# The table that turns S5 inputs into states, formed with steps and channels on the partitions instead of with states on the partitions and transposed afterwards

## The chip, the cores and the metric

The kernel runs on one core of a Trainium2 chip. The metric is the device time of one execution in microseconds (us). TensorE (PE) does the matrix products and the transposes, VectorE (DVE) and ScalarE (ACT) the work on elements, GpSimd (POOL) in this kernel mostly issues DMAs, and SyncE (SP) issues the loads of the weights. Each engine works through its own list of instructions in order; where one needs what another engine or a DMA makes, it waits on a semaphore.

## The reference

One inference step of a backbone of two layers (`DEPTH = 2`) with 1024 channels over 384 tokens, 128 of context and 256 latent. In each layer two half-step feed-forward networks (hidden width 2816) stand around a mixing block. One branch of the mixing block is a linear state-space layer (S5): 32 groups of 16 channels, each with 64 complex states, in both directions of time. Cut to it:

```python
def _s5_direction(u, a_re, a_im, log_dt, b_re, b_im, c_re, c_im, h0, reverse):
    dt = jnp.exp(log_dt)[:, None]
    mag = jnp.exp(a_re * dt)
    abar_r, abar_i = mag * jnp.cos(a_im * dt), mag * jnp.sin(a_im * dt)
    ...                                      # q = (abar - 1) / a
    bbar_r = qr[..., None] * b_re - qi[..., None] * b_im
    bbar_i = qr[..., None] * b_im + qi[..., None] * b_re
    bu_r = jnp.einsum('gph,blgh->blgp', bbar_r, u)
    ...
    _, _, sr, si = lax.associative_scan(_ssm_combine, (ar, ai, bu_r, bu_i), reverse=reverse, axis=1)
    y = jnp.einsum('ghp,blgp->blgh', c_re, sr) - jnp.einsum('ghp,blgp->blgh', c_im, si)
```

The scan is linear, so the kernel takes eight steps (`TC = 8`) of a group's 16 channels (`H`) at once, 128 numbers, and needs three tables for each group: one from the eight steps' inputs to the 128 states of both directions (`ms`, products of powers of `abar` with `bbar`), one from the states to the eight outputs (`my`, powers with `c`), and one from inputs to outputs inside the eight steps (`kall`, spread out to `mi`). None of the tables depends on the tokens; only the weights enter.

## The kernel before

**The stream of weights.** Every projection is cut into units of 512 KB (four blocks of 128 rows by 256 columns). SP loads a unit (`wr`), ACT copies its high part into `wh` (L126), DVE subtracts to get the low part `wl` (L105), and PE does three products for each block, 24 matrix products a unit (`mm3`, L198 to L200). The pool of `wh` and `wl` has three buffers, so the `wh` of unit u+3 cannot be written before PE has finished unit u, and `next_unit` asks for the unit two ahead (`LOOK = 2`, L173). I number the units of the program from 0; the layers' first feed-forward network, in which layer 0's tables are made, takes units 0 to 67.

**What sets the order.** PE's list is in the order in which the code is written (L61). The lists of DVE, ACT, POOL and SP are ordered by a scheduler when the program is built; the weights' copies and subtractions have a higher priority there. After each unit `tick()` (L221) lets side programs go on by some steps: each is a Python generator, and what stands between two of its `yield`s is written into the program at that place. The side programs make the modulation vectors (`ax<-modw`, L386, with `modev` copies, L396) and the S5 tables. The tables' program goes on by 1.9 steps a unit in layer 0 and by 1.6 in layer 1.

**The tables.** `s5_params` (L788) forms the powers `pw` of `abar` and writes them in two orders to DRAM (`px`). `s5_tables` (L924) treats a layer's 32 groups in four rounds of eight (`GB`), each in two halves of four (`GS`). A round transposes `cr`, scales `braw` to `bb` (four products `cm` and two sums), and copies `bb` into the zero-padded `bp`. A half then makes `my` in six DVE operations of 128x512, and `mt`, the to-state table with the states on the partitions, in six more. Three steps later come the half's PE work: the responses (`tb<-my,bp`, L1024, and L1034, copied to `kall`, L1042) and eight transposes of `mt` (L138), which ACT copies to `ms` (L1050). POOL issues the DMAs of all of this: 33 in a round (8 loads, 2 of `my`, 2 of `ms`, 12 of `kall`, 9 that spread it to `mi`).

Of the kernel before, what the change touches and what calls it, by code (L numbers as in the profile page):

```python
# [19 lines left out]
P = 128  # L20
# [14 lines left out]
G = 32  # L35
# [21 lines left out]
def hybrid_step(ctx: ExitStack, tc: tile.TileContext, I, pos_r, pos_c, y_prompt, y_sample, new_state):  # L57
# [31 lines left out]
    def c4(shape, name):  # L89
        return sp.tile(shape, F32, tag="c4", name=name, bufs=5)  # L90
# [4 lines left out]
    def c2(shape, name):  # L95
        return sp.tile(shape, F32, tag="c2", name=name, bufs=7)
# [4 lines left out]
    def s1(shape, name):  # L101
        return sp.tile(shape, F32, tag="s1", name=name, bufs=7)
# [616 lines left out]
    px_d = [drm.tile([P, 2, 2, TC, G], F32, tag=f"px{l}", name=f"px{l}") for l in range(DEPTH)]  # L719
# [68 lines left out]
    def s5_params(raw, ldt):  # L788
# [81 lines left out]
        lo_i = slice(TC - 1, None, -1), slice(1, TC + 1)  # L870
        hi_i = slice(0, TC), slice(TC, 0, -1)
        for w in range(2):
            px = c4([P, DEPTH, 2, TC, G], "px")
            for i in range(2):
                for rows, ix in ((LO, lo_i[w]), (HI, hi_i[w])):
                    src = pw[rows, i, ix, :].rearrange("p n (l g) -> p l n g", l=DEPTH)
                    for l in range(DEPTH):
                        act.activation(px[rows, l, i], src[:, l], AF.Copy)
            for l in range(DEPTH):
                q.dma_start(px_d[l][:, w], px[:, l])  # L880
# [43 lines left out]
    def s5_tables(l):  # L924
        q = nc.gpsimd
        px = []
        for w in range(2):
            t = c2([P, 2, TC, G], "pxl")
            q.dma_start(t, px_d[l][:, w])
            px.append(t)  # L930
        psx, pyx = px
# [18 lines left out]
        for gb in range(G // GB):  # L950
# [9 lines left out]
            pool.memset(bb, 0.0)  # L960
# [5 lines left out]
            pool.memset(bp, 0.0)  # L966
# [4 lines left out]
            ts_(nci, cT[:, 1], -1.0)  # L971
            if gb + 1 < G // GB:
                nxt = load_bc(gb + 1)
            kall = s1([P, 2, 9 * H], "kall")
            for sb in range(GB // GS):
                s0 = sb * GS

                def pexp(tab, i):
                    v = tab[:, i, :, g0 + s0 : g0 + s0 + GS]
                    return v.rearrange("p n g -> p g n").unsqueeze(3).to_broadcast(sh)  # L980
# [5 lines left out]
                b_r, b_i = vec(bb[:, 0]), vec(bb[:, 1])  # L986
                my = c4([P, GS, 2, TC, H], "my")
                t1, t2 = c2(sh, "tp1"), c2(sh, "tp2")
                mul(t1, pexp(pyx, 0), c_r)
                mul(t2, pexp(pyx, 1), c_i)  # L990
# [3 lines left out]
                mul(t1, pexp(pyx, 1), c_r)  # L994
                yield
                mul(t2, pexp(pyx, 0), c_i)
# [10 lines left out]
                mt = c4([P, GS, 2, TC, H], "mt")  # L1007
                t1, t2 = c2(sh, "tp1"), c2(sh, "tp2")
                mul(t1, pexp(psx, 0), b_r)
                mul(t2, pexp(psx, 1), b_i)  # L1010
                yield
                sub(mt[:, :, 0], t1, t2)
                t1, t2 = c2(sh, "tp1"), c2(sh, "tp2")
                mul(t1, pexp(psx, 0), b_i)
                yield
                mul(t2, pexp(psx, 1), b_r)
                add(mt[:, :, 1], t1, t2)
                for _ in range(3):
                    yield
# [833 lines left out]
```

## Time and profile before

| | us |
|---|---|
| median of three runs | 1774.3 (1772.38 to 1775.49) |
| the profiled execution's own time | 1775.03 |
| its span in the trace | 1773.0 |
| PE busy | 1743.7 (98%) |
| DVE busy | 1246.8 (70%) |
| ACT busy | 795.8 (45%) |
| POOL busy | 203.5 (11%) |
| PE's waits for the subtraction `wl` | 4.2, in 5 waits |
| mean granted clock of TensorE | 0.997 |

The span is the time from the first to the last record; the execution's own time is 2.03 us longer. Busy shares are means over the whole program. PE's records are modelled at their ends and overlap, so that the step from one start to the next, and not the length of a record, tells how long a matrix product holds the engine: here 0.17 to 0.18 us, so that a unit of 24 takes about 4.1 us.

### The profile page before, as it was taken

What the parts mean: (1) busy time and instruction counts of PE and PEld (TensorE: products, weight loads), DVE (VectorE), ACT (ScalarE), POOL (GpSimd) and SP (SyncE); (2) the same over time, 40 slices, a digit from 0 to 9 for tenths busy, and PEclk for the clock granted to TensorE, in tenths of its full rate; (3) what the DMA queues carried; (4) which work ended last, traced back from release to release, by engine and by line L of the source; (5) the groups of instructions that cost most, each with busy time, mean ns of one, the idle gap of its engine ahead of it and who ended that gap; (6) DMA issues with size and microseconds to landing.
All of it is one profiled execution on the core that took longest, in us unless ns stands there. A gap on an engine that the chain in (4) does not pass through costs nothing.

```text
span 1773.0 us, 30946 instructions
## 1 busy us (share of the span) xinstructions
PE 1743.7 (98%) x12116; PEld 1652.8 (93%) x12116; DVE 1246.8 (70%) x2344; ACT 795.8 (45%) x1330; POOL 203.5 (11%) x400
## 2 busy tenths in 40 slices
PE   7999999999999999999999999999999999999997
PEld 4899999999999989999999899999999999999997
DVE  5496676778986885678487666767799788544435
ACT  3344333575355553233366233336744546423233
POOL 2012343310010000000001133232100000000000
PEclk9999999999999999999999999999999999999999
DMA  9778788776753677788346776667666443444332
GB/s 343 249 224 275 231 252 269 226 198 190 240 157 108 186 238 228 237 280 257 112 131 208 234 224 215 175 195 233 162 210 200 131 123 116 132 130 127 123 125 77
DMA packets 253753, 344.48 MB, mean 194 GB/s; under 512 B 22399, under 2 KB 216651, under 8 KB 253608
## 3 DMA queue, kind: packets, MB, share of 16 engines
q1 hardware_dynamic: 228504, 299.18, 53.4%
q0 software_dynamic: 17088, 39.51, 7.5%
q10 hardware_dynamic: 8016, 3.82, 0.8%
q8 instruction: 95, 1.56, 0.4%
q14 instruction: 50, 0.41, 0.1%
HBM read 309.75 MB, written 32.70 MB: 193 GB/s over the span
## 4 chain that ended last, share of the span: by engine, by line
PE 81%; DVE 10%; ACT 4%; DMA 3%; issue 2%; SPq 0%; ACTq 0%; DVEq 0%
PE mm L198 25%; PE mm L200 25%; PE mm L199 25%; PE ax L386 3%; DVE wl L105 3%; DVE cacc L123 2%; DMA wr<-in_w_gate_dram 1%; DVE m_t L105 1%; PE tb L138 1%; ACT wh L126 1%; DVE m_hh L105 1%; DMA modw<-in_w_mod_dram 1%; DVE macc L123 1%; DMA wr<-in_w_in_dram 1%; ACT zp L1125 0%
## 5 line engine op out<-in xcount | busy, mean ns | idle before, releaser
L105 DVE TENSOR_TENSOR wl<-wr,wh 128x1024 fp32r<-128x1024 f32 (+2 forms) x389 | 457.0, 1175 | 352.1 <-ACT wh L126 347.4
L126 ACT ACTIVATE wh<-wr 128x1024 fp32r<-128x1024 f32 (+1 forms) x387 | 395.9, 1023 | 613.9 <-PE mm L199 443.9
L198 PE MATMUL mm<-hh,wh 128*128 128x384 f32 x1840 | 625.3, 340 | 2.7 <-ACT hh L621 2.7
L200 PE MATMUL mm<-hh,wl 128*128 128x384 f32 x1840 | 617.1, 335 | 4.4 <-DVE wl L105 4.2
L199 PE MATMUL mm<-hl,wh 128*128 128x384 f32 x1840 | 616.3, 335 | 0.5 <-DVE hl L105 0.3
L198 PEld LDWEIGHTS mm<-hh,wh 128*128 128x128 f32 x1840 | 345.9, 188 | 31.7 <-issue 18.1
L200 PEld LDWEIGHTS mm<-hh,wl 128*128 128x128 f32 x1840 | 345.8, 188 | 6.7 <-DVE wl L105 6.7
L199 PEld LDWEIGHTS mm<-hl,wh 128*128 128x128 f32 x1840 | 345.9, 188 | 1.2 <-DVE hl L105 1.1
L198 PE MATMUL mm<-ah,wh 128*128 128x384 f32 x800 | 273.2, 342 | 0.0
L199 PE MATMUL mm<-al,wh 128*128 128x384 f32 x800 | 269.4, 337 | 0.8 <-DVE al L105 0.8
L200 PE MATMUL mm<-ah,wl 128*128 128x384 f32 x800 | 270.0, 338 | 0.0
L198 PEld LDWEIGHTS mm<-ah,wh 128*128 128x128 f32 x800 | 150.2, 188 | 10.2 <-issue 6.7
L199 PEld LDWEIGHTS mm<-al,wh 128*128 128x128 f32 x800 | 150.4, 188 | 1.7 <-DVE al L105 1.1
L200 PEld LDWEIGHTS mm<-ah,wl 128*128 128x128 f32 x800 | 150.2, 188 | 0.0
L123 DVE SCALAR_TENSOR_TENSOR x<-mm,gt,x 128x128 f32<-128x128 f32 x224 | 83.1, 411 | 33.3 <-PE mm L200 33.1
L198 PE MATMUL mm<-xh,wh 128*128 128x386 f32 x240 | 84.7, 353 | 0.0
L126 ACT ACTIVATE ah<-av 128x384 fp32r<-128x384 f32 x82 | 42.1, 519 | 89.4 <-DVE av L105 89.1
L200 PE MATMUL mm<-xh,wl 128*128 128x386 f32 x240 | 81.9, 341 | 0.0
L199 PE MATMUL mm<-xl,wh 128*128 128x386 f32 x240 | 81.9, 341 | 0.0
L123 DVE SCALAR_TENSOR_TENSOR macc<-modw,silu_c,macc 128x1024 f32<-128x1024 f32 x56 | 69.9, 1278 | 14.9 <-DMA modw<-in_w_mod_dram 14.9
L123 DVE SCALAR_TENSOR_TENSOR cacc<-pad,pv,cacc 128x399 f32<-128x399 f32 x120 | 69.7, 627 | 0.0
L386 PE MATMUL ax<-modw,silu_c 128*32 128x512 f32 (+1 forms) x576 | 63.2, 511 | 0.7 <-DMA modw<-in_w_mod_dram 0.7
(316 smaller groups left out, 1820.0 us busy)
## 6 DMA issues: line engine op xcount, KB each, us to landing
wr<-in_ffn_w_dram SPq DMA_DIRECT2D x256, 512.0 KB, 3.6
modw<-in_w_mod_dram SPq DMA_DIRECT2D x144, 512.0 KB, 5.4
wr<-in_w_gate_dram SPq DMA_DIRECT2D x48, 512.0 KB, 3.8
wr<-in_w_in_dram SPq DMA_DIRECT2D x24, 512.0 KB, 3.6
my<-my POOLq DMA_DIRECT2D x16, 512.0 KB, 5.5
ms<-ms POOLq DMA_DIRECT2D x16, 512.0 KB, 4.9
m_ms<-ms SPq DMA_DIRECT2D x16, 512.0 KB
m_my<-my SPq DMA_DIRECT2D x16, 512.0 KB, 7.4
```

The lines of the kernel that those rows point to most:

```text
L105: (eng or dve).tensor_tensor(out, a, b, op=op)
L123: dve.scalar_tensor_tensor(out, a, s, b, op0=op0, op1=op1)
L126: act.activation(hi, full, AF.Copy)
L138: pe.transpose(out, in_, ident[:rows, :rows])
L198: pe.matmul(out, wh[:, k, cols], xh, start=first, stop=False)
L199: pe.matmul(out, wh[:, k, cols], xl, start=False, stop=False)
L200: pe.matmul(out, wl[:, k, cols], xh, start=False, stop=last)
L386: pe.matmul(b[32 * s : 32 * s + 32, :w], silu_c[:, k, :], raws[i][:, c : c + w], start=(k == 0), stop=(k == KD - 1), skip_group_check=True,)
```

## The change

The to-state table is no longer transposed; its factors are. Once for the program, `pw` is transposed (eight transposes, four ACT copies into `pws`) and written to DRAM (`pt_d`, eight DMAs). In each round `factor_rows` copies `bb` to `bc` on ACT, transposes it (two transposes), copies the result to `bts` on ACT and writes it eight times to DRAM, once for each step (`btr_d`). In each half `to_rows_in` reads the powers with each row repeated for 16 partitions (`pt`, eight DMAs of 64 KB) and the repeated `bts` (`bt`, one DMA of 512 KB), and `to_rows` multiplies them on DVE in six operations of 128x512, straight into `ms`. The zeros of `bb` and `bp` are written by DVE in place of POOL, and only where they are needed. The second order of the powers (`psx`) is gone, and the `s1` pool has nine buffers instead of seven. POOL's DMAs in a round go from 33 to 59. A round has 16 steps instead of 17; the responses of a half come one or two steps after its `my` (before, at least five), and the factor's transposes three steps after `bb` is written into the program.

```diff
     def s1(shape, name):
-        return sp.tile(shape, F32, tag="s1", name=name, bufs=7)
+        return sp.tile(shape, F32, tag="s1", name=name, bufs=9)
...
-    px_d = [drm.tile([P, 2, 2, TC, G], F32, tag=f"px{l}", name=f"px{l}") for l in range(DEPTH)]
+    px_d = [drm.tile([P, 2, TC, G], F32, tag=f"px{l}", name=f"px{l}") for l in range(DEPTH)]
+    pt_d = [drm.tile([2, TC, G, P], F32, tag=f"pt{l}", name=f"pt{l}") for l in range(DEPTH)]
+    btr_d = [drm.tile([TC, H, G, 2 * P], F32, tag=f"btr{l}", name=f"btr{l}") for l in range(DEPTH)]
...
+        pws = c4([P, TC, P], "pws")
+        for i in range(2):
+            b = tb_bank()
+            for m in range(TC // 2):
+                transpose(
+                    b[:, m * P : (m + 1) * P], pw[:, i, 2 * m : 2 * m + 2, :].rearrange("p n r -> p (n r)"), P
+                )
+            bv = b.rearrange("p (m s) -> p m s", s=P)
+            o = pws[:, 4 * i : 4 * i + 4]
+            act.activation(o[:, ::-1, LO], bv[:, :, LO], AF.Copy)
+            act.activation(o[:, :, HI], bv[:, :, HI], AF.Copy)
+            yield
+        for n2 in range(2):
             for l in range(DEPTH):
-                q.dma_start(px_d[l][:, w], px[:, l])
+                r = n2 * NG + l * G
+                rows_d = pt_d[l].rearrange("i j g s -> (i j) g s")
+                for half, off in ((LO, 1 - n2), (HI, n2)):
+                    q.dma_start(
+                        rows_d[off::2, :, half].rearrange("m g s -> g m s"), pws[r : r + G, :, half]
+                    )
         yield
...
             bb = c2([P, 2, GB, 2 * H], "bb")
-            pool.memset(bb, 0.0)
+            dve.memset(bb[:, :, :, H:], 0.0)
...
             bp = c2([P, 2, GB, 2 * H], "bp")
-            pool.memset(bp, 0.0)
+            dve.memset(bp[LO, :, :, H:], 0.0)
+            dve.memset(bp[HI, :, :, :H], 0.0)
...
             nci = s1([P, GB, H], "nci")
             ts_(nci, cT[:, 1], -1.0)
+            bc = s1([P, 2, GB, H], "bc")
+            act.activation(bc, bb[:, :, :, :H], AF.Copy)
             if gb + 1 < G // GB:
                 nxt = load_bc(gb + 1)
+
+            def factor_rows():
+                b = tb_bank()
+                for i in range(2):
+                    transpose(b[:, i * P : (i + 1) * P], bc[:, i].rearrange("p g h -> p (g h)"), P)
+                bts = s1([P, 2, P], "bts")
+                act.activation(bts.rearrange("p i s -> p (i s)"), b[:, : 2 * P], AF.Copy)
+                for j in range(TC):
+                    q.dma_start(btr_d[l][j, :, gs].rearrange("h g x -> g h x"), bts.rearrange("r i s -> r (i s)"))
+
...
-                mt = c4([P, GS, 2, TC, H], "mt")
-                t1, t2 = c2(sh, "tp1"), c2(sh, "tp2")
-                mul(t1, pexp(psx, 0), b_r)
-                mul(t2, pexp(psx, 1), b_i)
+
+            def to_rows_in(sb):
+                gr = slice(g0 + sb * GS, g0 + (sb + 1) * GS)
+                pt = c4([P, 2, GS, P], "pt")
+                for j in range(TC):
+                    q.dma_start(pt[j * H : (j + 1) * H], pt_d[l][:, j, gr].unsqueeze(0).to_broadcast([H, 2, GS, P]))
+                bt = c4([P, GS, 2 * P], "bt")
+                q.dma_start(bt, btr_d[l].rearrange("j h g x -> (j h) g x")[:, gr])
+                bt = bt.rearrange("p g (i s) -> p g i s", s=P)
+                ins.append((pt, bt))
+
+            def to_rows(sb):
+                pt, bt = ins[sb]
+                ms = c4([P, GS, 2, P], "ms")
+                t1, t2 = (c2([P, GS, P], f"tp{i}") for i in (1, 2))
+                mul(t1, pt[:, 0], bt[:, :, 0])
+                mul(t2, pt[:, 1], bt[:, :, 1])
                 yield
-                sub(mt[:, :, 0], t1, t2)
-                t1, t2 = c2(sh, "tp1"), c2(sh, "tp2")
-                mul(t1, pexp(psx, 0), b_i)
+                sub(ms[:, :, 0], t1, t2)
+                t1, t2 = (c2([P, GS, P], f"tp{i}") for i in (1, 2))
+                mul(t1, pt[:, 0], bt[:, :, 1])
                 yield
-                mul(t2, pexp(psx, 1), b_r)
-                add(mt[:, :, 1], t1, t2)
-                for _ in range(3):
-                    yield
+                mul(t2, pt[:, 1], bt[:, :, 0])
+                add(ms[:, :, 1], t1, t2)
+                q.dma_start(ms_d[l][:, g0 + sb * GS : g0 + (sb + 1) * GS], ms)
+                yield
...
                 act.activation(kall[:, sb, :], b[:, : 9 * H], AF.Copy)
-                ms = c4([P, GS, 2, P], "ms")
-                for g2 in range(0, GS, 2):
-                    b = tb_bank()
-                    for j in range(4):
-                        transpose(
-                            b[:, j * P : (j + 1) * P], mt[:, g2 + j // 2, j % 2].rearrange("p i h -> p (i h)"), P
-                        )
-                    act.activation(ms[:, g2 : g2 + 2].rearrange("p g r c -> p (g r c)"), b, AF.Copy)
-                q.dma_start(ms_d[l][:, g0 + s0 : g0 + s0 + GS], ms)
+
+            mys, ins = [], []
+            yield
+            for n, _ in enumerate(from_rows(0)):
+                if n == 1:
+                    factor_rows()
+                yield
+            for n, _ in enumerate(from_rows(1)):
+                if n == 0:
+                    responses(0)
+                yield
+            to_rows_in(0)
+            yield
+            responses(1)
+            yield
+            to_rows_in(1)
+            yield from to_rows(0)
+            yield from to_rows(1)
             for s in range(4):
                 r = 32 * s
```

**Where the order differs on PE.** First the end of a half in before: the matrix products of `modw` belong to the modulation vectors, the rest to the tables.

```order
L386 MATMUL ax<-modw,silu_c 32x512 x4
L1024 MATMUL tb<-my,bp 32x128 x8
L1034 MATMUL tb<-cT,bb 32x16 x4
L1034 MATMUL tb<-nci,bb 32x16 x4
L138 MATMUL tb<-ident,mt 128x128 x8
L198 MATMUL mm<-ah,wh 128x384
```

In after, the responses stand alone at their place, and the transposes of a round come earlier. This is the place in layer 0's last round; the matrix product above it is the last of unit 54.

```order
L200 MATMUL mm<-hh_377,wl 128x384
L386 MATMUL ax<-modw,silu_c 32x512 x4
L138 MATMUL tb<-ident,bc 128x128 x2
L198 MATMUL mm<-hh_523,wh 128x384
L199 MATMUL mm<-hl_524,wh 128x384
```

The eight transposes of `mt` are gone from every half; two transposes of `bc` stand once in a round, directly behind a unit.

**Where the order differs on DVE.** Layer 0's last round, before: the scaling of `braw` (L105; `cm` are the products).

```order
L105 TENSOR_TENSOR wl<-wr,wh 128x1024
L105 TENSOR_TENSOR cm_3369<-q_t,braw 128x128
L105 TENSOR_TENSOR cm_3370<-q_t,braw 128x128
L105 TENSOR_TENSOR cm_3374<-q_t,braw 128x128
L105 TENSOR_TENSOR bb<-cm_3369,cm_3370 128x8x16
L105 TENSOR_TENSOR cm_3375<-q_t,braw 128x128
L105 TENSOR_TENSOR wl<-wr,wh 128x1024
L105 TENSOR_TENSOR bb<-cm_3374,cm_3375 128x8x16
```

The same place in after. The first row is the subtraction for unit 57, the unit three behind the one that PE finishes ahead of the transposes of `bc`.

```order
L105 TENSOR_TENSOR wl<-wr,wh 128x1024
L105 TENSOR_TENSOR ms<-tp_3219,tp_3220 128x4x128
L105 TENSOR_TENSOR ms<-tp_3260,tp_3261 128x4x128
L105 TENSOR_TENSOR tp_3297<-pt,bt 128x512
L105 TENSOR_TENSOR tp_3298<-pt,bt 128x512
L105 TENSOR_TENSOR tp_3302<-pt,bt 128x512
L105 TENSOR_TENSOR ms<-tp_3297,tp_3298 128x4x128
L105 TENSOR_TENSOR tp_3303<-pt,bt 128x512
L977 MEMSET bb 128x16x16
L105 TENSOR_TENSOR ms<-tp_3302,tp_3303 128x4x128
L105 TENSOR_TENSOR bb<-cm_3419,cm_3420 128x8x16
L105 TENSOR_TENSOR bb<-cm_3424,cm_3425 128x8x16
```

The sums that make `bb` now stand behind the subtraction for unit 57 and behind nine rows of the previous half's `ms`, where before they stood between two subtractions. ACT's copies into `bp` (four) and `bc`, which the transposes wait for, follow them; they stand behind ACT's copy `wh` for unit 57 as well.

## Rows read from the trace of the kernel before

**Rows 1.** The page: its head, busy times, and the chain by engine.
```profile
span 1773.0 us, 30946 instructions
...
PE 1743.7 (98%) x12116; PEld 1652.8 (93%) x12116; DVE 1246.8 (70%) x2344; ACT 795.8 (45%) x1330; POOL 203.5 (11%) x400
...
PE 81%; DVE 10%; ACT 4%; DMA 3%; issue 2%; SPq 0%; ACTq 0%; DVEq 0%
```

**Rows 2.** PE's waits: what for, us in total, times, longest.
```profile
PE ax L138 <- DMA crow<-in_c_dram: 5.3, 1, 5.3
PE mm L200 <- DVE wl L105: 4.2, 5, 1.4
...
PE ax L138 <- ACT modev L396: 0.5, 1, 0.5
```

**Rows 3.** Timeline of PE at a half's end: start, us, engine, line, names.
```profile
179.55 0.23 PE L1034 MATMUL tb<-nci,bb 128*32 128x16 f32 x8
179.71 1.24 PE L138 MATMUL tb<-ident,mt 128*128 128x128 f32 x8
180.71 0.42 PE L198 MATMUL mm<-hh,wh 128*128 128x384 f32 x1
```

**Rows 4.** Timeline of PE around a pair of transposes.
```profile
159.42 0.34 PE L200 MATMUL mm<-hh,wl 128*128 128x384 f32 x1
159.59 0.38 PE L138 MATMUL tb<-ident,cr 128*128 128x128 f32 x2
159.73 0.42 PE L198 MATMUL mm<-hh,wh 128*128 128x384 f32 x1
159.99 0.33 PE L199 MATMUL mm<-hl,wh 128*128 128x384 f32 x1
```

**Rows 5.** Timeline of PE, ACT and DVE at one unit's end.
```profile
173.37 0.34 PE L200 MATMUL mm<-hh,wl 128*128 128x384 f32 x1
173.62 1.06 ACT L126 ACTIVATE wh<-wr 128x1024 fp32r<-128x1024 f32 x1 [1.46 <-PE mm L199]
173.64 1.06 PE L386 MATMUL ax<-modw,silu_c 128*32 128x512 f32 x8
...
174.71 1.23 DVE L105 TENSOR_TENSOR wl<-wr,wh 128x1024 fp32r<-128x1024 f32 x1
```

**Rows 6.** DVE groups by shape: busy us, mean ns, idle before.
```profile
L105 DVE TENSOR_TENSOR wl<-wr,wh 128x1024 fp32r<-128x1024 f32 x355 | 433.7, 1222 | 318.2 <-ACT wh L126 313.4 <-PE ax L386 3.1
...
L105 DVE TENSOR_TENSOR tp<-pxl,bb 128x512 f32<-128x512 f32 x64 | 42.5, 685 | 0.4
...
L105 DVE TENSOR_TENSOR mt<-tp,tp 128x512 f32<-128x512 f32 x32 | 21.9, 685 | 0.2
...
L105 DVE TENSOR_TENSOR cm<-q_t,braw 128x128 f32<-128x128 f32 x32 | 7.8, 286 | 14.1 <-PE tb L138 10.1 <-DMA kd<-kall 4.0
...
L105 DVE TENSOR_TENSOR bb<-cm,cm 128x128 f32<-128x128 f32 x16 | 4.5, 284 | 0.0
```

**Rows 7.** ACT groups by shape.
```profile
L1050 ACT ACTIVATE ms<-tb 128x512 f32<-128x512 f32 x32 | 18.0, 599 | 2.5 <-PE tb L138 2.5
...
L969 ACT ACTIVATE bp<-bb 64x128 f32<-64x128 f32 x16 | 4.9, 307 | 0.2
...
L396 ACT ACTIVATE modev<-ax 128x512 f32<-128x512 f32 x5 | 2.9, 590 | 0.5 <-PE ax L386 0.5
L958 ACT ACTIVATE cT<-tb 128x256 f32<-128x256 f32 x8 | 2.9, 368 | 0.9 <-PE tb L138 0.9
```

**Rows 8.** Timeline of PE after a wait, with the idle time before it.
```profile
360.61 0.37 PE L468 MATMUL ax<-ones,sqacc 128*32 128x1 f32 x24 [1.96 <-DVE sqacc L105]
...
361.62 0.53 PE L198 MATMUL mm<-xh,wh 128*128 128x386 f32 x1
361.94 0.53 PE L199 MATMUL mm<-xl,wh 128*128 128x386 f32 x1
...
364.52 0.49 PE L198 MATMUL mm<-xh,wh 128*128 128x386 f32 x1
364.84 0.34 PE L199 MATMUL mm<-xl,wh 128*128 128x386 f32 x1
```

**Rows 9.** Windows: us, busy PE, PEld, DVE, ACT, POOL; PEclk, DMA share, GB/s.
```profile
362.00:364.00 2.00, 2.00 (x8) 2.00 (x7) 2.00 (x6) 0.00 (x0) 0.00 (x0) 0.50 0.66 198
```

**Rows 10.** The same view, layer 0's tables.
```profile
250.00:280.00 30.00, 30.00 (x210) 26.89 (x203) 26.08 (x48) 9.20 (x16) 13.81 (x25) 1.00 0.88 279
```

**Rows 11.** POOL groups by shape.
```profile
L1059 POOL DMA_DIRECT2D mib<-kd x64 | 33.6, 533 | 14.6 <-DMA kd<-kall 6.8 <-PE mm L200 3.3 <-issue 2.9
...
L1054 POOL DMA_DIRECT2D kd<-kall x32 | 16.5, 516 | 109.4 <-ACT kall L1042 102.8 <-DMA ms<-ms 6.5 <-issue 0.2
...
L942 POOL DMA_DIRECT2D cr<-in_s_c_re_dram x16 | 9.0, 566 | 4.1 <-DMA mib<-kd 2.1 <-DVE tp L105 1.8 <-issue 0.2
...
L960 POOL MEMSET bb<- 128x512 f32 x8 | 4.3, 532 | 20.2 <-DVE mt L105 20.2
```

**Rows 12.** DMA issues: KB each, median us to landing.
```profile
my<-my POOLq DMA_DIRECT2D x16, 512.0 KB, 5.5
ms<-ms POOLq DMA_DIRECT2D x16, 512.0 KB, 4.9
...
mib<-kd POOLq DMA_DIRECT2D x64, 64.0 KB, 5.6
```

More of the change, by code (lines that the diff above doesn't have):

```diff
@@ L868, in s5_params @@
             yield
[L870 to L878, printed above, removed]
-            for l in range(DEPTH):
-                q.dma_start(px_d[l][:, w], px[:, l])
+        px = c4([P, DEPTH, 2, TC, G], "px")
+        for i in range(2):
+            for rows, ix in ((LO, slice(1, TC + 1)), (HI, slice(TC, 0, -1))):
+                src = pw[rows, i, ix, :].rearrange("p n (l g) -> p l n g", l=DEPTH)
+                for l in range(DEPTH):
+                    act.activation(px[rows, l, i], src[:, l], AF.Copy)
+        for l in range(DEPTH):
+            q.dma_start(px_d[l], px[:, l])
+        yield
[12 more added lines that the diff above has]
+        for n2 in range(2):
+            for l in range(DEPTH):
+                r = n2 * NG + l * G
[4 more added lines that the diff above has]
+                    )
         yield
@@ L925, in s5_tables @@
         q = nc.gpsimd
[L926 to L931, printed above, removed]
+        pyx = c2([P, 2, TC, G], "pxl")
+        q.dma_start(pyx, px_d[l])
         def load_bc(gb):
@@ L971, in s5_tables, with from_rows, pexp @@
             ts_(nci, cT[:, 1], -1.0)
+            bc = s1([P, 2, GB, H], "bc")
+            act.activation(bc, bb[:, :, :, :H], AF.Copy)
             if gb + 1 < G // GB:
                 nxt = load_bc(gb + 1)
+            def factor_rows():
+                b = tb_bank()
+                for i in range(2):
+                    transpose(b[:, i * P : (i + 1) * P], bc[:, i].rearrange("p g h -> p (g h)"), P)
[3 more added lines that the diff above has]
+                    q.dma_start(btr_d[l][j, :, gs].rearrange("h g x -> g h x"), bts.rearrange("r i s -> r (i s)"))
             kall = s1([P, 2, 9 * H], "kall")
-            for sb in range(GB // GS):
+            def from_rows(sb):
                 s0 = sb * GS
-                def pexp(tab, i):
-                    v = tab[:, i, :, g0 + s0 : g0 + s0 + GS]
+                def pexp(i):
+                    v = pyx[:, i, :, g0 + s0 : g0 + s0 + GS]
                     return v.rearrange("p n g -> p g n").unsqueeze(3).to_broadcast(sh)
@@ L985, in s5_tables @@
                 c_r, c_i = vec(cT[:, 0]), vec(cT[:, 1])
-                b_r, b_i = vec(bb[:, 0]), vec(bb[:, 1])
                 my = c4([P, GS, 2, TC, H], "my")
+                mys.append(my)
                 t1, t2 = c2(sh, "tp1"), c2(sh, "tp2")
-                mul(t1, pexp(pyx, 0), c_r)
-                mul(t2, pexp(pyx, 1), c_i)
+                mul(t1, pexp(0), c_r)
+                mul(t2, pexp(1), c_i)
                 yield
@@ L993, in s5_tables @@
                 t1, t2 = c2(sh, "tp1"), c2(sh, "tp2")
-                mul(t1, pexp(pyx, 1), c_r)
+                mul(t1, pexp(1), c_r)
                 yield
-                mul(t2, pexp(pyx, 0), c_i)
+                mul(t2, pexp(0), c_i)
                 stt(
@@ L1006, in s5_tables, with responses @@
                 yield
[L1007 to L1010 removed]
+            def to_rows_in(sb):
[13 more added lines that the diff above has]
+                mul(t2, pt[:, 1], bt[:, :, 1])
                 yield
[L1012 to L1014 removed]
+                sub(ms[:, :, 0], t1, t2)
+                t1, t2 = (c2([P, GS, P], f"tp{i}") for i in (1, 2))
+                mul(t1, pt[:, 0], bt[:, :, 1])
                 yield
[L1016 to L1019 removed]
+                mul(t2, pt[:, 1], bt[:, :, 0])
+                add(ms[:, :, 1], t1, t2)
+                q.dma_start(ms_d[l][:, g0 + sb * GS : g0 + (sb + 1) * GS], ms)
+                yield
+            def responses(sb):
+                s0 = sb * GS
+                my = mys[sb]
                 b = tb_bank()
```

1 line of the change is left out of this document (added).

## The prediction, made before the changed kernel ran

> **What bounds the kernel now.** I read the page first. PE is busy for 1743.7 of 1773.0 us, 98%, and the chain that ended last runs through PE for 81% [rows 1]. Then the list of PE's waits: the largest is for a load at the start (5.3 us), the next 4.2 us in five pieces for `wl`, and the one for `modev` is 0.5 us; no line names a table tile, neither `mt` nor `my` nor `kall` [rows 2]. So the tables cost PE today only the instructions that they put into its list, and DVE, ACT and POOL work beside it. A change of the tables can gain what leaves PE's list, and can lose wherever PE has to wait for a table where now it does not.
>
> **What leaves PE's list.** At a half's end the eight transposes of `mt` start at 179.71 and the next matrix product at 180.71: 1.00 us [rows 3]. There are 16 halves (two layers, four rounds, two halves): 16.0 us. What comes in is a pair of transposes in each of eight rounds. The pair in before stands between two matrix products that start at 159.42 and, the second behind it, at 159.99, 0.57 us for what would be two steps of 0.17 to 0.18 (159.42 to 159.59 is one): 0.22 us [rows 4], in eight rounds 1.8 us. The eight transposes of `pw`, in two groups of four, cost about as much as one half's eight and one switch more, 1.2 us. The saving is 16.0 - 1.8 - 1.2 = 13.0 us.
>
> **What the other engines do.** DVE's six products and sums of a half stay six of the same size; the 685 ns of `tp` and `mt` hold for `tp<-pt,bt` and `ms` too [rows 6]. ACT loses two copies of 599 ns in a half [rows 7] and gains small ones. POOL loses 16 memsets of 532 ns and gains 26 DMAs in a round, each some 0.53 us of issue [rows 11]. DVE has 30% of the span free, ACT 55%, POOL 89% [rows 1], so the amounts hide beside PE. The edits at the start (one order of powers less, `pws`) lie there too; if they came late, the whole first round would, which is in the range's upper end. The DVE memsets, smaller than POOL's of 512 columns, I take at 0.25 us, near the 0.286 of `cm`, a 128x128 operation [rows 6]; between 0.1 and 0.53 the sum moves by 2 us at most.
>
> **What PE waits for.** Here the order decides, not the amounts. The copy `wh` of unit u+3 waits for PE to end unit u. One such hand-over stands in the trace: the last product of a unit starts at 173.37 and lasts to 173.71, `wh` ends at 174.68, 0.97 us later, and `wl` runs from 174.71 to 175.94, 2.23 us later [rows 5]. As long as PE has units u+1 and u+2 ready, nobody waits. But where PE, straight after unit u, meets an instruction that needs something which on ACT stands behind `wh` of u+3, or on DVE behind `wl` of u+3, PE stops for 0.97 or 2.23 us plus all that lies between, because it cannot go on to u+1 past that instruction. In before the transposes of `mt` come several steps behind their last sum, and the list of waits shows that this never decides. I went through the two lists of after for every place where PE needs a table, with the unit that PE has finished and the last unit whose `wh` or `wl` stands ahead of what it needs. Where they are one or two apart there is no wait. They are three apart here:
>
> Four times at a round's pair of transposes (layer 0 behind units 45 and 54, layer 1 behind 232 and 242), with the previous half's `ms` in between. For unit 54 the DVE rows are shown with the change: behind `wl` of unit 57 come eight operations of 0.685 us, 5.5 us; the memset, 0.25; two `bb` of 0.284, 0.6 [rows 6]. Then ACT copies `bp` four times at 0.307, 1.2, and `bc`, of 128x256 like `cT` with 0.368, 0.4 [rows 7]. From the unit's end that is 2.2 + 5.5 + 0.25 + 0.6 + 1.2 + 0.4 = 10.15 us; half of a `modw` step, whose eight products take 1.00 us (173.64 to the next product; its row is [rows 5]), lies beside it: 9.6 us. At unit 45 it is 10.0 by the same count, since residual sums stand in between; at 232, 9.5; at 242 part of the `ms` rows are already done, 7.3. Together 36.4 us.
>
> In layer 0's second round: behind unit 37 `bc` stands behind `wh` of unit 40, 0.97 + 1.2 + 0.4 = 2.6 us; behind unit 38 the responses need `my`, two operations behind `wl` of unit 41, 2.23 + 1.37 = 3.6; behind unit 40 a bank that `bts` frees, 0.97 + 0.37 = 1.3. Three times (units 44, 65, 241) the modulation's transposes wait for `modev`, 590 ns [rows 7], behind `wh`: 0.97 + 0.59 = 1.6 each, 4.7. In layer 1 two or three waits of 0.3 to 0.5 us: 0.8. Together 13.0 us.
>
> **What a wait costs behind it.** In before PE waited 1.96 us, and from 361.62 to 364.84 ten products start 0.32 us apart instead of 0.175 [rows 8]; the granted clock of 362 to 364 is 0.50, the level of 1.2 GHz [rows 9]. That is 10 x 0.147 = 1.5 us for one drop. Six of the waits above are longer than 1.96 us: 9.0 us. The others are shorter; 1.4 us, the longest for `wl` [rows 2], left the clock up. The Trainium skill ("TensorE: Matmul & The Clock Gate", HAM oscillation — how this bites in real kernels) says that waits between groups of products can send the array back to its lower clock every time; the row at 362 agrees for one wait. By that rule taken for the four waits of 1.3 to 1.6 us too, 6 us more would be lost, 1826 in all; I keep the rows' 9.0.
>
> **The sum.** 36.4 + 13.0 + 9.0 - 13.0 = 45.4 us slower. On the profiled execution's 1775.0 us (its span and 2.0 around it) that is 1820.4; the median of the runs is 0.7 lower, so 1820.
>
> **Rivals.**
>
> *No new wait decides.* If what PE needs were always two units behind, or the lists ran so far ahead that the needed copy was done in time, only the saving would be left: 1774.3 - 13.0 = 1761, faster. For it speaks that before has many of the same steps and no such wait [rows 2], and that DVE and ACT have idle time. Against it: idle time does not help an instruction that stands behind a `wl` whose buffer PE itself still reads. It decides if the distance at the long places is two, not three. Half way, with the long waits gone and the short ones kept, it is 1761 + 13 + 3, some 1777, within noise of before. I give 0.09 to the first and 0.04 to the second.
>
> *Transfers come late.* Factors now pass through DRAM: `bts` is written eight times, then `bt` read, then DVE multiplies. Bounded by the nearest rows, a small transfer on POOL lands in 5.6 us (`mib`) and one of 512 KB in 4.9 to 5.5 [rows 12], so the chain is about 11 us behind `bts`, and ahead of it POOL issues at 0.53 us each: 8 writes, 8 + 1 reads and whatever of `my` and the old round stands before them, some 10 to 14 us. Between `bts` and the first `tp<-pt,bt` lie seven to eight steps, at 1.9 a unit four units or 17 us in layer 0 and 20 in layer 1; that is tight. If `bt` is late, DVE stands, and `wl` of the next units stands behind it; up to 4 us in each of eight rounds, 32 us more: 1850. For it: in 250 to 280 the DMA engines are at 0.88 with 279 GB/s [rows 10], and the change adds some 13 MB a layer to what passes there (8 x 128 KB of writes a round, twice 1 MB of reads). Against it: POOL is idle for most of the span, and DVE reaches those rows late anyhow, behind the waits above. 0.22. The Trainium skill ("DMA: Bandwidth & Descriptors", Anatomy of one DMA — SWDGE) gives 2.0 us plus the bytes at 436 GB/s; as an estimate by that page the two transfers would take 2.3 + 3.2 = 5.5 us, and this rival would be gone. The rows, 4.9 to 5.6 for one, are longer, and I go by them.
>
> *The waits overlap.* A long wait at the pair of transposes gives DVE and ACT time to catch up, so that the short waits of the same round vanish, and the clock falls less often: 36.4 + 4 + 6 - 13 = 33, 1808. This is the lower part of the likeliest case, not a case apart.
>
> **How the numbers follow.** The forecast, waits that decide by order, has 0.65, with a range of its own of 1800 to 1838; late transfers 0.22, 1832 to 1865; none or only short waits 0.13. A range from 1792 to 1850 leaves out the last 0.12 and the upper part of the second. Within 0.2%, 3.5 us, is what a measurement of this kernel can't tell from no change. Faster by more than that: 0.09; within: 0.04; slower: 0.87.
>
> **What would show it.** In the profile of after, PE's waits should name `ACT bc` for L138 with about 36 to 40 us in all, four of them 7 to 10 us long, and `DVE my`, `ACT modev` with a few us each. The granted clock should fall behind the long ones. PE's busy time at full clock should be 13 us shorter, its list 104 transposes shorter. If L138 waits for `bc` only for a few us in all, the count of units is wrong, and so is the sign. If DVE's idle time before `tp<-pt,bt` is large and its releaser is the DMA of `bt`, the second rival has it. If the sum is right but in other places, the prediction is right by luck.

## The result: 1841.5 us after 1774.6, and the profile after

The changed kernel takes 1841.51 us in the median (1839.73 to 1846.21), the kernel before 1774.57: a ratio of 1.0383, 95% interval 1.0361 to 1.0405. The profiled execution took 1840.74 us, its span 1839.0. The forecast was 1820 with a range of 1792 to 1850. The time lies above the range of the likeliest case alone (1800 to 1838) and inside that of late transfers (1832 to 1865), so the time by itself doesn't tell which of the two it was; the waits have to.

The page of after, the lines that answer to [rows 1]:

```profile
span 1839.0 us, 30960 instructions
...
PE 1750.2 (95%) x12012; PEld 1658.6 (90%) x12012; DVE 1253.8 (68%) x2368; ACT 783.1 (43%) x1310; POOL 309.9 (17%) x596
...
PE 65%; DVE 9%; DMA 5%; issue 3%; POOL 1%; ACT 1%; DVEq 0%; ACTq 0%; POOLq 0%
```

The span is 66.0 us longer, PE's busy time only 6.5. So PE stands still for 88.8 us instead of 29.3. The list of PE's waits in after (what for, us in total, times, longest) names what [rows 2] doesn't have, the tables:

```profile
PE tb L138 <- ACT bc L991: 35.1, 4, 13.4
PE ax L138 <- ACT modev L396: 13.4, 4, 6.1
PE ax L468 <- DVE sqacc L105: 5.4, 2, 4.1
...
PE tb L1072 <- DVE my L105: 3.0, 1, 3.0
PE tb L1072 <- DVE my L123: 2.4, 1, 2.4
...
PE tb L1072 <- ACT bts L1000: 1.3, 1, 1.3
```

The timeline gives each wait its place. The same count of units as in the prediction, with its price and the measured one:

| PE waits behind unit | for | forecast | measured |
|---|---|---|---|
| 37, 38, 40 | bc, my, a bank behind bts | 2.6, 3.6, 1.3 | 3.10, 2.97, 1.29 |
| 44, 65, 241 | modev | 1.6 each | 1.45, 5.28, 6.12 |
| 45, 54, 232, 242 | bc, behind the old round's ms | 10.0, 9.6, 9.5, 7.3 | 9.41, 13.42, 9.19, none |
| layer 1's responses | my | 0.8 in all | 2.42 |
| sum | | 49.4 | 54.7 |

Other waits grew by 4.9 us in all; a new one of 4.1 is for `sqacc`, the sums of squares at layer 1's mixer, while the one of 1.96 in layer 0 [rows 8] is gone. PE's list lost 104 transposes, and its busy time still rose by 6.5. If the saving was the 13.0 us forecast, 19.5 us went to half clock: 54.7 + 4.9 + 19.5 - 13.0 = 66.1. The last two terms are not measured apart here, so that the sum must close. The run without the passage, below, has the same list of PE and 1727.8 us of it busy; against that run it is 22.4 us for the clock and 15.9 for the saving, some 1.5 of which are the drop at 362 [rows 8] that this run doesn't have.

The wait behind unit 54, across engines (start, duration, engine, line, names, idle before):

```profile
321.44 1.22 DVE L105 TENSOR_TENSOR wl<-wr,wh 128x1024 fp32r<-128x1024 f32 x1
322.58 1.29 DVE L105 TENSOR_TENSOR ms<-tp,tp 128x512 f32<-128x512 f32 x2
...
328.56 1.90 DVE L105 TENSOR_TENSOR tp<-pt,bt 128x512 f32<-128x512 f32 x3 [4.70 <-DMA bt<-btr]
...
330.38 0.68 DVE L105 TENSOR_TENSOR ms<-tp,tp 128x512 f32<-128x512 f32 x1
...
332.40 0.48 DVE L105 TENSOR_TENSOR bb<-cm,cm 128x128 f32<-128x128 f32 x2
332.71 0.31 ACT L986 ACTIVATE bp<-bb 64x128 f32<-64x128 f32 x1 [11.74 <-DVE bb L105]
...
334.00 0.42 ACT L991 ACTIVATE bc<-bb 128x256 f32<-128x256 f32 x1
...
334.47 0.69 PE L138 MATMUL tb<-ident,bc 128*128 128x128 f32 x2 [13.42 <-ACT bc L991]
```

This is the order shown with the change, in time: `wl` of unit 57, eight products and sums for the previous round's `ms`, of both its halves, then `bb`, `bp`, `bc`, then PE. Two things are new. DVE stood 4.70 us for `bt`, and by the forecast's own prices PE's 13.42 us are 9.6 and this, less a little. The wait for `modev` behind unit 241, forecast at 1.6 us:

```profile
1204.18 1.28 DVE L105 TENSOR_TENSOR ms<-tp,tp 128x512 f32<-128x512 f32 x2
...
1204.90 0.38 ACT L396 ACTIVATE modev<-ax 128x256 f32<-128x256 f32 x1 [4.71 <-DVE ms L105]
...
1205.34 0.69 PE L138 MATMUL ax<-ident,modev 128*128 128x128 f32 x2 [6.12 <-ACT modev L396]
```

`modev` did not wait for ACT's `wh`, but for DVE's `ms`: it takes a buffer of the pool that `tp` uses (L395), and the sums that free one stand late on DVE.

The clock, by windows (us, busy PE, PEld, DVE, ACT, POOL; granted clock, DMA share, GB/s): behind the wait of 3.10 us that ends at 219.14, and behind the one that ends at 334.47.

```profile
218.00:220.00 2.00, 0.86 (x6) 0.86 (x7) 1.99 (x5) 1.04 (x4) 2.00 (x5) 1.00 1.00 377
220.00:222.00 2.00, 2.00 (x13) 2.00 (x12) 1.78 (x3) 0.00 (x0) 1.86 (x3) 1.00 0.89 333
336.00:338.00 2.00, 2.00 (x8) 2.00 (x7) 0.03 (x1) 0.00 (x0) 2.00 (x4) 0.50 0.31 78
338.00:340.00 2.00, 2.00 (x8) 2.00 (x7) 0.56 (x1) 0.37 (x1) 2.00 (x5) 0.50 0.58 167
```

The clock had fallen to 0.50, the level of 1.2 GHz, during the long wait (the windows from 324 to 334 have 0.50 too), and it stayed there for more than 5 us of PE's work; behind the 3.10 us it did not fall.

### The profile page after: what moved, and what is told of

Read it like the earlier page. It is cut to its first block, busy times and chain, and to the rows that moved or that the text cites. A ratio compares the mean times of both kernels' runs of the same rounds, so it can differ in the third digit from the quotient of the medians.

```text
span 1839.0 us, 30960 instructions
## 1 busy us (share of the span) xinstructions
PE 1750.2 (95%) x12012; PEld 1658.6 (90%) x12012; DVE 1253.8 (68%) x2368; ACT 783.1 (43%) x1310; POOL 309.9 (17%) x596
## 4 chain that ended last, share of the span: by engine, by line
PE 65%; DVE 9%; DMA 5%; issue 3%; POOL 1%; ACT 1%; DVEq 0%; ACTq 0%; POOLq 0%
PE mm L198 21%; PE mm L200 20%; PE mm L199 20%; DVE cacc L123 2%; DVE wl L105 2%; DMA bt<-btr 1%; PE ax L386 1%; DVE m_t L105 1%; DMA my<-my 1%; DVE m_hh L105 1%; DMA wr<-in_w_in_dram 1%; DMA kd<-kall 1%; DVE macc L123 1%; DMA modw<-in_w_mod_dram 0%; ACT wh L126 0%
## 5 line engine op out<-in xcount | busy, mean ns | idle before, releaser
L105 DVE TENSOR_TENSOR wl<-wr,wh 128x1024 fp32r<-128x1024 f32 (+2 forms) x389 | 457.4, 1176 | 394.5 <-ACT wh L126 385.2
L198 PEld LDWEIGHTS mm<-hh,wh 128*128 128x128 f32 x1840 | 349.7, 190 | 30.8 <-issue 16.4
L199 PEld LDWEIGHTS mm<-hl,wh 128*128 128x128 f32 x1840 | 349.6, 190 | 1.5 <-DVE hl L105 1.4
L1043 POOL DMA_DIRECT2D pt<-pt x128 | 64.7, 510 | 61.8 <-DMA pt<-pt 18.7
```

Source lines behind the costliest of these rows:

```text
L105: (eng or dve).tensor_tensor(out, a, b, op=op)
L198: pe.matmul(out, wh[:, k, cols], xh, start=first, stop=False)
L199: pe.matmul(out, wh[:, k, cols], xl, start=False, stop=False)
L1043: q.dma_start(pt[j * H : (j + 1) * H], pt_d[l][:, j, gr].unsqueeze(0).to_broadcast([H, 2, GS, P]))
```

## The experiments

The theory by then: the factors' passage through DRAM takes longer than the steps between give it, so the products of a half are placed on DVE among the next round's work, and whatever PE needs of that round stands behind them. The rival: the new places alone (transposes three steps, responses one or two behind what they need) make PE wait, whatever the transfers do. Each kernel is the changed one with the edit shown, unless said otherwise; ratios are against before.

**Without the passage.**

```diff
-                for j in range(TC):
-                    q.dma_start(pt[j * H : (j + 1) * H], pt_d[l]...)
+                pool.memset(pt, 0.0)
...
-                q.dma_start(bt, btr_d[l]...)
+                pool.memset(bt, 0.0)
...
-                for j in range(TC):
-                    q.dma_start(btr_d[l][j, :, gs]..., bts...)
+                q.dma_start(btr_d[l][0, :, gs]..., bts...)
```

> The changed kernel with the factors' passage through DRAM left out: the tiles of the two factors are filled with zeros by POOL in place of their 18 reads in a round, and seven of the eight writes of the transposed factor are gone; so the to-state table is zero. Everything else is issued as in the changed kernel (the transposes, the copies, the products, the responses at their places). Theory (the transfers are late, the scheduler therefore puts the products of a half among those of the next round, and PE waits for what stands behind them): the ten table waits of 54.7 us and the clock drops behind them go, only the saving of 13 us stays: 1762 us (1758 to 1768). Rival (the waits come from the places alone, transposes three steps and responses one or two steps behind what they need): the waits for bc and my stay, 1820 to 1842.

Measured 1759.78 us, ratio 0.9914 (0.9899 to 0.9929). Its page and PE's waits:

```profile
span 1759.2 us, 30767 instructions
...
PE 1727.8 (98%) x12012; PEld 1639.3 (93%) x12012; DVE 1251.7 (71%) x2368; ACT 782.2 (44%) x1310; POOL 231.8 (13%) x428
```

```profile
PE ax L138 <- DMA crow<-in_c_dram: 5.2, 1, 5.2
PE mm L200 <- DVE wl L105: 4.8, 6, 1.6
...
PE ax L138 <- ACT modev L396: 0.5, 1, 0.5
```

Not one wait for a table is left, at the same places in the program: PE's list is that of after, row for row. Places alone don't make PE wait; the rival is out. What differs beside the transfers is the order on DVE and ACT, whose lists were made anew when this kernel was built. The same place in DVE's list, from the subtraction for unit 56 on:

```profile
293.55 1.23 DVE L105 TENSOR_TENSOR wl<-wr,wh 128x1024 fp32r<-128x1024 f32 x1 [3.16 <-ACT wh L126]
294.70 0.28 DVE L105 TENSOR_TENSOR bb<-cm,cm 128x128 f32<-128x128 f32 x1
```

The last sum of `bb` stands behind the subtraction for unit 56, two units after the one that PE finishes ahead of the transposes (54), not three. No product for `ms` lies between, here and in the other rounds. That the scheduler moves the products because it reckons with the transfers' time is inferred from such lists; the scheduler itself was not examined. With the transfers gone their traffic is gone too, which the next two runs part.

**Layer 1 paced slower.**

```diff
-            track(tables(1), 1.6, 8)
+            track(tables(1), 1.2, 0)
```

> The changed kernel with one number changed: layer 1's tables go on by 1.2 steps a unit from the first unit, not by 1.6 from the eighth, so that a round lasts 13.3 units (some 55 us) instead of 10 (41 us), with the same steps between any two things. Theory (the rounds are too short for the passage, which took 35 us from the transposed factor to its landing in layer 0's third round): layer 1's waits of 2.4, 9.2 and 6.1 us go with their clock drops of 2.6 to 3.1 us each: 1841.5 - 17.7 - 8.4 = 1815 us, down to 1811 if the wait for the sums of squares at layer 1's mixer shrinks too. Rival (places alone): no change, 1838 to 1845. Rival (traffic on POOL's queue slows the weights' loads): at most 5 us less, 1836.

Measured 1819.77 us (1.0243, 1.0221 to 1.0264). That is some 5 us above the theory's 1815 and below both rivals. Its waits name layer 0's places only; in layer 1 the timeline has none for a table any more, and no product for `ms` stands between the last subtraction and `bb` there. `sqacc` at layer 1's mixer still costs 2.38 us.

```profile
PE tb L138 <- ACT bc L991: 27.0, 3, 12.9
PE ax L138 <- ACT modev L396: 7.2, 3, 5.3
...
PE tb L1072 <- DVE my L105: 3.4, 2, 3.0
```

**Both layers paced slower.** Layer 0 has no spare units, so the parameters and rotations go two steps at a time to make room for the rounds.

```diff
-        yield from s5_rotations(l)
+        yield from by(s5_rotations(l), 2)
-            yield from s5_params(*s5_params_in(nc.gpsimd))
+            yield from by(s5_params(*s5_params_in(nc.gpsimd)), 2)
-            track(tables(0), 1.9, 8)
+            track(tables(0), 1.15, 0)
-            track(tables(1), 1.6, 8)
+            track(tables(1), 1.2, 0)
```

> As the kernel with layer 1 paced at 1.2, and in layer 0 the rounds paced at 1.15 steps a unit from the start instead of 1.9 from the eighth unit; to make room the parameters and rotations ahead of the rounds go two steps at a time. The to-state table is made as in the changed kernel, all transfers included. Theory (round time against passage time): no wait for a table is left, so the time is that of before less the 13 us saved on PE, 1762 us, up to 1768 with waits at the denser start: faster than before. Rival (places alone): 1835 to 1845. Rival (the 26 more transfers in a round cost by their traffic alone): above 1774.

Measured 1776.99 us (1.0013, 1.0003 to 1.0023). The table waits are down to 2.5 us, as the theory has it: with all transfers in place and only more time for them, 64.5 of the 67 us are gone. DVE stood 13.5 us for `pt` and `bt` here, more than the 7.3 in after, and PE hardly noticed: in DVE's list `bb` stands ahead of these products. So the order in the list is what PE pays for, more than the landing itself. The time, though, is 9 us above the theory's range and where the second rival, the traffic alone, had put it (above 1774): the 13 us on PE don't show. In the profiled execution, the longest of ten (1781.56 us), PE waited 5.6 us for `srow`, the mixer's load of the cached state, which stood behind the tables' transfers, and 3.7 us for `sqacc`, behind a weight load that came 4.6 us late.

**The next round's factor placed earlier.**

```diff
...
+            made = prep(gb + 1) if gb + 1 < G // GB else None
             yield from to_rows(0)
```

`prep` holds what makes `cT`, `bb`, `bp`, `nci` and `bc`.

> The changed kernel with the next round's scaled factor (bb, bp, bc, cT) written into the program ahead of the previous round's products, one place earlier; pace and transfers unchanged. Theory (passage late): the four waits for bc, 35.1 us, vanish by this place, but my of the next round still stands behind the previous round's products on DVE, so PE waits for my at three responses for 6 to 9 us each: 1841.5 - 35 - 8 + 24 + 6 = 1828 us (1815 to 1840). Rival (only the place of bb matters): the waits for bc and their clock go and nothing comes in their stead, 1795 to 1800.

Measured 1829.69 us (1.0317, 1.0294 to 1.034): near the 1828 expected, in part by luck: three waits for `my` of 6 to 9 us were priced, and there were three of 10.5 to 10.7 and one of 2.9.

```profile
PE tb L1078 <- DVE my L105: 34.8, 4, 10.7
PE ax L138 <- ACT modev L396: 13.3, 4, 6.3
```

The 35.1 us for `bc`, with 5.4 for `my` beside them, became 35.0 us for `my` (0.2 of it in a line not shown): what PE asks for first has changed, and DVE's products for `ms` still stand ahead of it.

**A buffer of its own for `modev`.** The second line is changed at both places where `modev` is made, and the `s1` pool loses a buffer.

```diff
-        return sp.tile(shape, F32, tag="s1", name=name, bufs=9)
+        return sp.tile(shape, F32, tag="s1", name=name, bufs=8)
-        ev = sp.tile([P, 512], F32, tag="c2", name="modev", bufs=7)
+        ev = sp.tile([P, 512], F32, tag="ev", name="modev", bufs=1)
```

> The changed kernel with the modulation's copy modev in a buffer of its own instead of the pool that the products tp use (the s1 pool has eight buffers instead of nine to make room). Theory (modev waits for a buffer that the late sums of ms free, and PE waits 1.5, 5.3 and 6.1 us for modev): these 12.9 us and the clock drops of 1.9 and 2.7 us behind them go: 1841.5 - 17.5 = 1824 us (1820 to 1830). Rival (modev is late because it stands behind wh on ACT, as the prediction said): 3 us at most, 1837 to 1843.

Measured 1842.64 us (1.0371, 1.0348 to 1.0394): no gain, a miss of 18 us.

```profile
PE tb L138 <- ACT bc L991: 47.4, 5, 13.0
PE ax L468 <- DVE sqacc L105: 8.1, 3, 3.5
```

The waits for `modev` are gone but for the 0.5 us that before has too, which shows what it waited for; but `bc` rose from 35.1 to 47.4 us in five waits. One is 3.6 us longer (behind unit 45), and the fifth is 9.27 us behind unit 242, the place where the forecast had 7.3 and after had none: there `modev`, one unit earlier, had waited for the same `ms`. DVE's list was built anew here as well (ahead of `bb` for unit 242 it has one more subtraction than in after), and what the missing `s1` buffer does to it was not run apart.

**One write instead of eight.** The factor's rows stand channel first, so that one DMA with a repeating source reaches all eight copies; the layouts of `bc` and `btr_d`, changed for it, are not shown.

```diff
-                for j in range(TC):
-                    q.dma_start(btr_d[l][j, :, gs].rearrange("h g x -> g h x"), bts.rearrange("r i s -> r (i s)"))
+                q.dma_start(
+                    btr_d[l][gb].rearrange("j h g x -> (h g) j x"),
+                    bts.rearrange("r i s -> r (i s)").unsqueeze(1).to_broadcast([P, TC, 2 * P]),
+                )
```

> The changed kernel at its own pace, with the transposed factor written by one DMA instead of eight. Theory (the passage is long because bts waits for a buffer, and because reads queue behind it; the eight writes are 4.8 of its 35 us): the 4.7 us that DVE waited for bt in layer 0's last round go, and little else: 1836 us (1828 to 1841). Rival (the number of POOL's DMAs makes the passage long): below 1815.

Measured 1831.24 us (1.0322, 1.0309 to 1.0335): 10 us better, DVE's wait for `bt` down from 4.7 to 1.0 us, the waits for `bc` to 31.9. The number of DMAs is a part of the passage, not the whole. The passage itself in after, layer 0's third round (its transposes start at 275.17):

```profile
292.75 0.36 ACT L1000 ACTIVATE bts<-tb 128x256 f32<-128x256 f32 x1
...
293.41 0.64 POOL L1002 DMA_DIRECT2D btr<-bts  x1 [6.76 <-ACT kall L1090]
...
301.61 2.58 POOL L1043 DMA_DIRECT2D pt<-pt  x5
...
309.24 0.57 POOL L1045 DMA_DIRECT2D bt<-btr  x1
...
318.92 0.50 POOL L1043 DMA_DIRECT2D pt<-pt  x1 [2.42 <-DMA bt<-btr]
...
320.27 0.56 POOL L1045 DMA_DIRECT2D bt<-btr  x1 [0.84 <-PE mm L200]
```

`bts` is copied 17.6 us after its transposes, and no transfer holds it up on the chip: ACT's list has the copies `wh` of three units (281.35, 286.43 and 291.79) ahead of it, and no row shows the buffer that the theory names. POOL issues the eight writes until 298, the reads wait in its list for earlier DMAs to land, and the second `bt`, issued at 320.27, is what DVE waits for until 328.56.

**The saving alone**, from before: the transposes of `mt` and ACT's copies left out.

```diff
-                ms = c4([P, GS, 2, P], "ms")
-                for g2 in range(0, GS, 2):
...
-                q.dma_start(ms_d[l][:, g0 + s0 : g0 + s0 + GS], ms)
+                q.dma_start(ms_d[l][:, g0 + s0 : g0 + s0 + GS], mt.rearrange("p g r i h -> p g r (i h)"))
```

> The kernel before with the transposes of mt and ACT's copies of them left out; the table is written untransposed, so it holds the right numbers in the wrong order. It measures the saving alone. Theory (1.00 us a half): 1774.6 - 16.0 = 1758.6 us (1757 to 1761). Rival (PE's transposes hide beside something else, or the freed ACT copies shift another wait): 1765 or more.

Measured 1760.49 us (0.9923, 0.9905 to 0.994), 13.7 us by the ratio with an interval of 10.6 to 16.9; PE's busy time fell from 1743.7 to 1726.6. Consistent with 16.0.

**Pacing without the change**, from before: the two-at-a-time start, 1.2 and 1.25 steps a unit.

> The kernel before with the same pacing (layer 0 at 1.2 steps a unit from the start with the parameters and rotations two steps at a time, layer 1 at 1.25 from the start), its table formed and transposed as before; its rounds have one step more, hence 1.2 and 1.25. Theory (before had no table wait, so room gives it nothing): 1774 us (1770 to 1780). Rival (the pacing itself is what gains, by a better order elsewhere): 1760 to 1768.

Measured 1790.87 us (1.009, 1.0075 to 1.0105), which neither expected.

```profile
PE mm L200 <- DVE wl L105: 8.1, 8, 2.4
...
PE ax L138 <- DMA wr<-in_ffn_w_dram: 5.1, 1, 5.1
PE tb L138 <- DVE mt L105: 3.2, 2, 2.0
```

At 115 us, in the denser start, PE waits 5.1 us to transpose `rows`; the profile puts it down to a weight load, though the instruction reads `rows`, whose own load was issued at 105.8. 3.2 us are waits for `mt` at the end of layer 0. So pacing is no gain in itself. Not all of its 16 us were traced.

**Towards a version that beats both.** Four runs tried to take the paced kernel's rest away: `srow` in a tile of its own, then its load moved to SP, then the one write in addition, and last, without it, layer 0 at 1.25 steps a unit. The edit shows the first two together.

```diff
-        srow = s1([P, 2, PS, 2], "srow")[:G]
-        gq.dma_start(srow, I["state_ssm"]...)
+        srow = sp.tile([P, 2, PS, 2], F32, tag="srow", name="srow", bufs=1)[:G]
+        tq.dma_start(srow, I["state_ssm"]...)
```

> The kernel with both layers paced, and the cached state (srow) in a tile of its own, so that its load needn't wait for a buffer of the tables' pool. In the kernel with both layers paced PE waited 5.6 us for that load, and ran some 3.0 us longer at half clock behind it. Theory (no table wait is left; what remains above 1762 us are the mixer's loads that the tables' last transfers delay): 1777.0 - 5.6 - 3.0 = 1768 us (1764 to 1772), so 0.2 to 0.5% faster than before. Rival (the load is late for the POOL queue, not for its buffer): 1777.

> The kernel with both layers paced and srow in a tile of its own, with srow's load issued by SP instead of POOL. In the kernel without this, POOL reached the load only at 397.9 us, behind the table's transfers, and PE waited 5.3 us for it, with 1.5 us at half clock behind. Theory (the load's place in POOL's list): 1775.1 - 5.3 - 1.5 = 1768 us (1765 to 1771), 0.4% faster than before. Rival (the next thing of the mixer, U or sgw, comes as late and takes the wait over): 1773 to 1776.

> As the kernel with both layers paced and srow on SP, and the transposed factor written by one DMA of 1 MB that repeats it eight times, instead of eight of 128 KB (its rows stand channel first so that one pattern reaches them): POOL issues 52 DMAs a round instead of 59. Theory (shorter passage, the tables' last transfers end some 5 us earlier, ahead of the mixer's loads): 1766 us (1761 to 1770). Rival (a large write delays the weights' loads more than eight small ones): above the kernel without it by 2 us or more.

> As the kernel with both layers paced and srow on SP, but layer 0's tables at 1.25 steps a unit instead of 1.15, so that they end some four units earlier, ahead of the mixer's own loads; two of layer 0's modulation vectors at 0.46 instead of 0.4, so that modev isn't needed beside the last round. Theory (what is left above 1762 us are the mixer's loads and its U, which the tables' last transfers delay: 5.8 and 2.1 us with 1.9 us at half clock): 1775.4 - 9.8 + 2 for a shorter wait at the mixer's first operand = 1767 us (1763 to 1771), faster than before. Rival (U and the loads are late for the traffic of the mixer itself, or the wait moves on): 1773 to 1778.

Measured 1775.07 (0.9996, 0.9986 to 1.0007), 1775.36 (0.9999, 0.9988 to 1.0009), 1774.68 (1.0005, 0.9995 to 1.0014) and 1779.75 us (1.0029, 1.0018 to 1.0039). No theory came true. In the first two the rival has the time; the third lies between theory and rival, and the last is slower than both. In the traces the wait moved on each time. In the second of them:

```profile
PE tb L1234 <- issue: 5.8, 1, 5.8
...
PE ax L468 <- DVE sqacc L105: 4.3, 3, 2.0
...
PE tb L138 <- ACT bc L996: 2.3, 2, 1.6
PE tb L138 <- DMA sgw<-in_sg_w_dram: 2.1, 1, 2.1
```

`srow` came in time, and the mixer's first product with `U` waited 5.8 us instead; the profile names no releaser there, and names `U`'s load for 5.6 us at the same place in the third. In the last, U and `sgw` came in time, and PE waited 3.1 us for the mixer's first operand `xl`, with 3.0 us at half clock. No version that keeps the whole computation beats the kernel before beyond its interval. Without the passage the time was 1759.8. The paced kernels lose about the whole saving again, at the mixer's start, where the tables' last transfers meet the mixer's loads, and at half clock behind these waits, as far as these rows tell. That sum was not closed by a run, and the cost of the pacing itself, 16 us in before, was not taken apart from it.

## Why the prediction was right, and where its sizes were not

**The mechanism** was right and was shown: PE meets a table instruction behind a unit, what it needs stands behind that unit's third successor on DVE or ACT, and PE stops. At nine of the ten single places that it named PE waited; in layer 1's responses, where it had two or three short waits, there was one of 2.42. 49.4 us were forecast and 54.7 measured. The sizes came out less well, and the range had room for it: of the 21.5 us by which 1841.5 misses 1820, 5.3 are in these waits, 4.9 in waits that the sum left out, and the clock has most of the rest.

**Why the order is so** the prediction did not say. It set the order against late transfers as two causes. The runs tie them together: take the transfers away, or give them more time, and the lists come out with `bb` ahead of the old round's products, and the waits go. The second rival (up to 32 us of DVE standing for `bt`) was right as a cause and wrong as a price: DVE stood 7.3 us for `bt` and `pt` in all. Its passage of 21 to 25 us, counted from `bts`, was 35 to 36 us in layer 0's third round (292.75 to 328.3), and 53 from the transposes, since `bts` stood 17.6 us in ACT's list. The Trainium skill ("DMA: Bandwidth & Descriptors", Anatomy of one DMA — SWDGE) would have the two transfers at 2.3 and 3.2 us, as an estimate by its fit; the medians here are 4.9 us for a write of `bts` and 7.9 for `bt`. The measurement decides, and the page's figure would have spoken against the rival.

**The step that was mis-sized most** is the clock: 9.0 us forecast as six drops of 1.5, some 20 measured (19.5 with the forecast's saving, 22.4 against the run without the passage). There were more drops, nine between the start and the end, where before has one. Four stand behind waits whose drop the sum had priced; the others stand behind the two long waits for `modev`, the 2.42 us in layer 1, and two waits that are not for tables (2.3 and 4.1 us). A drop cost up to 3 us where I had priced all by the one at 362 [rows 8]. The Trainium skill ("TensorE: Matmul & The Clock Gate", HAM oscillation — how this bites in real kernels) tells of a kernel whose waits between groups of products re-throttle the array every time; taken as a rule for the short waits too it gave 15 us, nearer in size. The trace doesn't agree every time: the waits of 1.29, 1.45 and 3.10 us left the clock at 1.00.

**The price of `modev`**, 1.6 us each from `wh` and its own duration [rows 5, 7], was 1.5 at the first place and 5.3 and 6.1 at the others. The step took the last `wh` ahead of it as its only wait, and left out the buffer that it needs.

**The wait behind unit 242** didn't come. The last subtraction ahead of `bb` there is that of unit 244, two after 242 and not three as the prediction counted, with twelve rows of the old round between. They ran from 1201.78 to 1209.3, while PE stood for `modev` until 1205.34 and then worked through unit 242 partly at half clock; `bc` was ready at 1211.3 and PE came at 1212.2. With `modev` out of the way the wait was there, though in a list built anew. The sum treated two waits for one chain of work as two.

**The saving** of 13.0 us was about right: the time without the passage is 15 us below before, and 16.0 us for the transposes alone is inside the interval of the run that leaves them out.

## What to carry to other kernels

Where an engine works through a list in order and its operands come through buffers that it frees itself, count for every new wait how many units stand between the wait and the last unit ahead of its operand on the other engine: where it was all three buffers here, with work of another kind in between, the wait was paid, though DVE was busy for only 68% of the time. Work that is moved off such an engine and through DRAM needs the whole passage's time between its ends, buffers and queue included: what has too little of it can be put among the next round's work in another engine's list. A run without the passage tells its price at once. Waits that hang on one chain of work do not add up, and removing the one that is listed only brings out the next.

## What was not expected of the hardware

A wait of 3.10 us on PE left its clock at full, one of 2.97 us seven microseconds later did not (the clock was 0.50 in 228 to 230), and in before 1.96 us were enough [rows 8, 9]. The same wait of 3.10 us was followed by 0.50 in the run with layer 1 paced slower (220 to 226), and one of 2.92 us, alone, in the run with the factor placed earlier. So the length of the wait alone does not tell; the runs don't show what does. The reads that repeat a DRAM row for 16 partitions landed in 7.0 us (median) for 64 KB; `mib`, of the same size, in 4.3 in the same kernel and 5.6 in before [rows 12]. Whether the repeating or the place in the queue makes the difference was not run apart. With them in its queue, `my` took 7.1 us instead of 5.5, and the weights of the mixer's first projection 5.7 instead of 3.6.
